# Two layers of a hybrid decoder trunk: every second pair of gate and up tiles begins with its 256-wide products, and down products stand inside a pair

## The chip, the cores and the metric

The kernel runs on one core of one Trainium2 chip. The metric is the device time of one execution in microseconds (us); lower is better. Three runs of the kernel before took 1044.72, 1044.97 and 1044.98 us, so its median is 1044.97 us. The profile shows one more execution, which has its own time, 1044.58 us.

The core has five engines that each work through their own list of instructions in order and wait for each other through semaphores: TensorE (PE in the profile: matrix products into the banks of PSUM; PEld is its loading of the stationary operand), VectorE (DVE), ScalarE (ACT), GpSimd (POOL) and SyncE (SP, which here only issues transfers). Main memory is read and written by DMA.

## What is computed

```
def swiglu(x, w_gate, w_up, w_down):
    return (jax.nn.silu(x @ w_gate) * (x @ w_up)) @ w_down
...
    for l in range(DEPTH):
        h = h + 0.5 * swiglu(rms_norm(h, ffn1_norm[l]), ffn1_w_gate[l], ffn1_w_up[l], ffn1_w_down[l])
        h = h + hybrid_mixer(rms_norm(h, mix_norm[l]), ...)
        h = h + 0.5 * swiglu(rms_norm(h, ffn2_norm[l]), ffn2_w_gate[l], ffn2_w_up[l], ffn2_w_down[l])
```

There are 256 tokens of width 1024, two layers (DEPTH is 2), and a hidden width of 2816 in each of the four feed-forward blocks (FFNs). All inputs are float32. The mixer (three groups of attention heads) is not touched by the change.

## The kernel before

Every float32 matrix is used as the sum of two parts in a reduced float32 format: the high part is the rounded value, the low part what is left. A product of two such matrices is three products: high by high, high by low, low by high.

**An FFN.** The hidden width is cut into 22 tiles of 128 (`NF`), counted by `f`. For each `f` there is a gate product (1024 by 128 weights against the tokens) and an up product of the same size; both have their own PSUM bank of 512 columns. Eight products that take the high weights as stationary operand and stream 512 columns (the tokens' high parts and their low parts side by side) fill the whole bank; these are the "wide" ones. Eight more, with the low weights and 256 columns (the tokens' high parts), add into the first half; these are the "narrow" ones. ScalarE then copies the second half of the bank out (`summed`, L434), VectorE adds the first half to it (L435), and from there the bank is free. Gate: times `norm.rb` (L439), a tanh on ScalarE (L441), two VectorE steps (`silu`, L458 and L459). Up: copy and add as before, times the gate (L446), then the high part (`hh`, L449) and the low part (`hl`, L452) of hidden tile `f`.

**The down product.** `down(k)` takes hidden tile `k` and its 128 rows of down weights and adds into four banks of tag "acc": 12 products of 512 columns, in the order high weights by `hh`, low weights by `hh`, high weights by `hl` for each bank. It runs four tiles late (`DOWN_LAG` is 4): beside pair `f` stands `down(f - 4)`. The last four are done in `tail` (or, in the very last FFN, in `finish`), bank after bank.

**Order.** The order of every engine's work is the order in which the program emits it. `Pair` (two weight tiles, two banks) emits gate wide, up wide, gate narrow, up narrow (`both`). Pairs are used from `f` = 2 on; in the first FFN from `f` = 6 on (`PAIR_FROM`), where tiles before stand singly (`proj`). In the loop over `f`, `both` comes first, then the gate's copy and the tanh, a `W.pump()`, then `down(f - DOWN_LAG)`, another pump, then the rest of the gate and the up side.

**Weights.** `Weights` loads raw float32 tiles through SP's queue (five buffers). A `pump` emits one high part on ScalarE (L117, tag "wh") and the low part of the unit before it on VectorE (L121, tag "wl"); eight buffers each. Units are taken in the order gate, up, down. So ScalarE and VectorE do two things in one list: they empty PSUM for the tile at hand, and they split weights for tiles to come. In the last two tiles (`late` in `hidden`) the pumps come after `hl`.

**Banks.** There are four banks of tag "gu", taken in turn, so pair `f` writes the banks that pair `f - 2` has left. In the first FFN, after `f` = 8, `aside` (`before_mixer`) takes two of them for two transposes (L177), and pair 9 then gets the banks of pair 8.

Of the kernel before, what the change touches and what calls it, by code (L numbers as in the profile page):

```python
# [21 lines left out]
KT = D // P  # L22
# [13 lines left out]
DOWN_LAG = 4  # L36
# [105 lines left out]
def kernel(ctx: ExitStack, tc: tile.TileContext, x, ffn1_norm, ffn1_w_gate, ffn1_w_up, ffn1_w_down,  # L142
# [17 lines left out]
    def bank(tag):  # L160
        return psum.tile([P, 512], F32, name="ps_" + tag, tag=tag)
# [43 lines left out]
    W = Weights(tc, raw_pool, split_pool)  # L205
# [87 lines left out]
    def mm(o, l, r, start, stop):  # L293
        T.matmul(o, l, r, start=start, stop=stop, skip_group_check=True)  # L294
# [64 lines left out]
    def tokens(o, q, hid, w, start, stop, cols=slice(0, 512)):  # L359

        t, c = q % 2, q // 2
        mm3(o, [h[:, t * P:(t + 1) * P] for h in hid], [v[:, 0, 512 * c + cols.start:512 * c + cols.stop] for v in w],
            start, stop)
# [8 lines left out]
    def ffn(norm, nxt, aside=None, g0=None):  # L372
        hid = {}

        def down(k):
            w = W.take()
            for q in range(4):
                tokens(acc[q], q, hid[k], w, k == 0, False)
            del hid[k]
# [16 lines left out]
        def proj(between=None, after=0, tag="gu"):  # L396


            w = W.take()
            ps = bank(tag).rearrange("p (a b) -> p a b", a=2)  # L400
            for k in range(KT):
                mm(ps, w[0][:, k], norm.x[:, k], k == 0, False)
            for k in range(KT):
                mm(ps[:, 0], w[1][:, k], norm.h[:, k], False, k == KT - 1)
                if between and k == after:
                    between()
            return ps

        class Pair:
# [11 lines left out]
            def narrow(self, ks):  # L421
                for w, ps in zip(self.ws, self.ps):
                    for k in ks:
                        mm(ps[:, 0], w[1][:, k], norm.h[:, k], False, k == KT - 1)

            def both(self, ks=range(KT)):
                self.wide(ks)
                self.narrow(ks)
                return self.ps

        def summed(ps):

            o = tmp(S)
            A.copy(o, ps[:, 1])  # L434
            V.tensor_tensor(o, ps[:, 0], o, op=ALU.add)  # L435
            return o

        def gated(t_):
            V.tensor_tensor(t_, t_, norm.rb, op=ALU.mult)  # L439
            th = tmp(S)  # L440
            A.activation(th, t_, AF.Tanh, scale=0.5)  # L441
            return t_, th

        def hidden(f, t_, th, u, pumps=1):
            late = f >= NF - 2
            V.tensor_tensor(t_, u, t_, op=ALU.mult)  # L446
            hh = hp.tile([P, S], F32R, name="hh", tag="hh")
            hl = hp.tile([P, S], F32R, name="hl", tag="hl")
            (V.tensor_copy if late else A.copy)(hh, t_)  # L449
            if not late:  # L450
                W.pump(pumps)
            V.tensor_tensor(hl, t_, hh.bitcast(F32), op=ALU.subtract)  # L452
            if late:
                W.pump(pumps)
            hid[f] = (hh, hl)

        def silu(t_, th):
            V.scalar_tensor_tensor(t_, th, 1.0, t_, op0=ALU.add, op1=ALU.mult)  # L458
            V.tensor_tensor(t_, t_, norm.rb, op=ALU.mult)  # L459

        first = g0 is not None
        early = {}
        if first:
# [4 lines left out]
            u1 = proj(norm.broadcast, 6)  # L468
# [25 lines left out]
        for f in range(1, NF):  # L494
            last = f == NF - 1
            paired = f >= (PAIR_FROM if first else 2)
            if paired:
                g, u = Pair().both()
            else:
                g, u = early[f] if f in early else proj(), u1 if f == 1 else None  # L500
            t_, th = gated(summed(g))
            if not last:
                W.pump()
            if f >= DOWN_LAG:
                down(f - DOWN_LAG)
                if not last:
                    W.pump()
            silu(t_, th)
            hidden(f, t_, th, summed(u or proj()), 3 if last else 1)
            if f == 8 and aside:  # L510
                aside()
# [567 lines left out]
    def before_mixer(l):  # L1079
        if l == 0:  # L1080
            turn_gains(1)
            turn_gains(2)
            V.tensor_copy(identr, ident)
            V.memset(causal[:, P:2 * P], 0.0)
            for t in range(2):
                V.tensor_scalar(causal[:, 2 * t * P:(2 * t + 1) * P], future, NEG, None, op0=ALU.mult)
        mixer_tables(l)
# [4 lines left out]
    norm = Norm(0, 0)  # L1092
# [52 lines left out]
    for l in range(DEPTH):  # L1145
        norm = ffn(norm, lambda: Norm(1, l), lambda: before_mixer(l), g0 if l == 0 else None)
        norm = mixer(l, norm, lambda: Norm(2, l))
        norm = ffn(norm, (lambda: Norm(0, l + 1)) if l + 1 < DEPTH else None)
# [35 lines left out]
```

## Time and profile before

| what | us |
|---|---|
| median of three runs | 1044.97 |
| the profiled execution, its time | 1044.58 |
| its span, first to last instruction | 1042.8 |
| PE busy | 1036.8 |
| DVE busy | 810.9 |
| ACT busy | 588.8 |
| the longest idle time of PE that the waits view shows inside the four FFNs | 0.6 |

The page of the profile gives busy times and shares of the span; groups of instructions stand as line, engine, operation, out<-in and count. In a timeline a row is a run of equal instructions: its start and its length in us, the engine, the line, what is written and read, the count, and in brackets the idle time of the engine before it with what ended it. The ends of matrix products are modelled, and products overlap, so that the distance between the starts of two rows, not the length of one, is the time that PE spent on the first.

### The profile page before, as it was taken

The page shows a single profiled execution, that of the slowest core. Times are in us where ns is not written, and L with a number is a line of the kernel's source. Part 1 is how long each engine was busy: PE and PEld are TensorE (multiplying, and loading weights), DVE is VectorE, ACT ScalarE, POOL GpSimd, SP SyncE. Part 2 cuts the span into 40 slices and gives each one's busy share as a digit, 9 for nine tenths or more (in the row PEclk, how much of TensorE's full clock was granted, in tenths as well). Part 3 has the DMA queues.
Part 4 walks back from the last instruction along what each step waited for, and adds up shares of the span by engine and source line. Part 5 has one row for each costly group of instructions (what it writes and reads, how often), then busy time and mean ns, then how long its engine had stood idle before and what let it go on. Part 6 is the DMA issues. An engine that isn't in the chain of part 4 may idle for free.

```text
span 1042.8 us, 15029 instructions
## 1 busy us (share of the span) xinstructions
PE 1036.8 (99%) x5667; PEld 900.4 (86%) x5667; DVE 810.9 (78%) x1536; ACT 588.8 (56%) x1047; POOL 143.5 (14%) x173
## 2 busy tenths in 40 slices
PE   9999999999999999999999999999999999999998
PEld 8888888898888888888888888888988888888887
DVE  4997777789876897777779777777898768877775
ACT  6665555667754665455466545547667555655551
POOL 1003000167700000000000210002765000000000
PEclk9999999999999999999999999999999999999999
DMA  9675555455441364554646574555455214574631
GB/s 326 213 242 177 194 207 170 157 196 192 149 137 41 122 236 169 201 192 171 202 162 203 170 240 159 205 164 192 162 186 178 81 60 153 193 240 151 214 121 40
DMA packets 130905, 181.68 MB, mean 174 GB/s; under 512 B 7009, under 2 KB 104721, under 8 KB 130833
## 3 DMA queue, kind: packets, MB, share of 16 engines
q1 hardware_dynamic: 130512, 180.65, 51.1%
q8 instruction: 44, 0.72, 0.3%
q14 instruction: 29, 0.23, 0.1%
q10 hardware_dynamic: 320, 0.08, 0.0%
HBM read 179.67 MB, written 1.05 MB: 173 GB/s over the span
## 4 chain that ended last, share of the span: by engine, by line
PE 92%; DVE 4%; ACT 2%; DMA 1%; issue 1%; SPq 0%; ACTq 0%
PE ps_gu L294 61%; PE ps_acc L294 28%; ACT wh L117 2%; DVE wl L121 1%; PE ps_acc L329 1%; DVE tmp L435 1%; PE ps_gu L943 1%; DMA trunk<-in_x_dram 1%; PE ps_gu L1045 1%; DVE tmp L459 0%; DVE tmp L446 0%; DVE tmp L439 0%; DVE tmp L458 0%; PE ps_acc L644 0%; ACT tmp L434 0%
## 5 line engine op out<-in xcount | busy, mean ns | idle before, releaser
L121 DVE TENSOR_TENSOR wl<-raw,wh 128x1024 fp32r<-128x1024 f32 (+2 forms) x343 | 416.5, 1220 | 26.4 <-ACT wh L117 26.1
L117 ACT CAST wh<-raw 128x1024 fp32r<-128x1024 f32 (+2 forms) x343 | 346.1, 1036 | 5.2 <-PE ps_gu L294 4.8
L294 PE MATMUL ps_gu<-xhl,wh 128*128 128x512 f32 (+1 forms) x1408 | 336.2, 389 | 1.2 <-DVE tmp L435 1.2
L294 PEld LDWEIGHTS ps_gu<-xhl,wh 128*128 128x128 f32 x1408 | 261.4, 188 | 55.5 <-DVE tmp L435 2.9
L294 PEld LDWEIGHTS ps_gu<-xhl,wl 128*128 128x128 f32 x1400 | 180.7, 191 | 7.2
L294 PE MATMUL ps_gu<-xhl,wl 128*128 128x256 f32 x1400 | 184.6, 283 | 0.0
L294 PE MATMUL ps_gu<-wh,xhl 128*128 128x512 f32 (+2 forms) x512 | 158.5, 379 | 0.0
L435 DVE TENSOR_TENSOR tmp<-ps_gu,tmp 128x256 f32<-128x256 f32 x175 | 73.6, 421 | 105.1 <-ACT tmp L434 104.9
L294 PE MATMUL ps_acc<-wh,hh 128*128 128x512 f32 (+1 forms) x352 | 137.7, 391 | 0.0
L294 PE MATMUL ps_acc<-wl,hh 128*128 128x512 f32 (+1 forms) x352 | 137.4, 390 | 0.0
L294 PE MATMUL ps_acc<-wh,hl 128*128 128x512 f32 (+1 forms) x352 | 136.5, 388 | 0.0
L434 ACT COPY tmp<-ps_gu 128x256 f32<-128x256 f32 x175 | 63.8, 365 | 92.4 <-PE ps_gu L294 91.9
L294 PEld LDWEIGHTS ps_gu<-wh,xhl 128*128 128x128 f32 x512 | 94.8, 188 | 14.5
L449 ACT CAST hh<-tmp 128x256 fp32r<-128x256 f32 x80 | 32.5, 407 | 125.9 <-DVE tmp L446 125.9
L294 PE MATMUL ps_gu<-wl,xhl 128*128 128x512 f32 (+2 forms) x256 | 95.7, 374 | 0.0
L441 ACT ACTIVATE tmp<-tmp 128x256 f32<-128x256 f32 x88 | 36.8, 418 | 82.0 <-DVE tmp L439 82.0
L305 POOL TENSOR_TENSOR y_n<-msq,minus_half 128x2 f32<-128x2 f32 x6 | 7.7, 1280 | 540.4 <-DVE msq L304 540.4
L294 PEld LDWEIGHTS ps_acc<-wh,hl 128*128 128x128 f32 x352 | 66.1, 188 | 14.1
L294 PEld LDWEIGHTS ps_acc<-wh,hh 128*128 128x128 f32 x352 | 66.4, 189 | 11.7
L294 PEld LDWEIGHTS ps_acc<-wl,hh 128*128 128x128 f32 x352 | 66.4, 189 | 10.8
L294 PEld LDWEIGHTS ps_gu<-wl,xhl 128*128 128x128 f32 x256 | 48.2, 188 | 6.6
L318 ACT ACTIVATE xhl<-ps_acc,gT 128x256 fp32r<-128x256 f32 x48 | 19.0, 474 | 37.5 <-PE ps_acc L329 37.0
(221 smaller groups left out, 1019.4 us busy)
## 6 DMA issues: line engine op xcount, KB each, us to landing
raw<-in_ffn_w_down_dram SPq DMA_DIRECT2D x44, 1024.0 KB, 5.0
raw<-in_ffn_w_gate_dram SPq DMA_DIRECT2D x43, 1024.0 KB, 6.9
raw<-in_ffn_w_up_dram SPq DMA_DIRECT2D x43, 1024.0 KB, 7.1
raw<-in_w_in_dram SPq DMA_DIRECT2D x24, 1024.0 KB, 5.0
raw<-in_w_out_dram SPq DMA_DIRECT2D x8, 1024.0 KB, 4.8
raw<-in_w_in_dram SPq DMA_DIRECT2D x4, 768.0 KB, 5.1
raw<-in_w_in_dram SPq DMA_DIRECT2D x4, 656.0 KB, 5.2
trunk<-in_x_dram SPq DMA_DIRECT2D x4, 256.0 KB, 5.1
```

Source lines behind the costliest of these rows:

```text
L117: self.nc.scalar.copy(hv, src)
L121: (engine or self.nc.vector).tensor_tensor(lv, self.srcs[self.n_low], hv.bitcast(F32), op=ALU.subtract)
L294: T.matmul(o, l, r, start=start, stop=stop, skip_group_check=True)
L305: G.tensor_tensor(y, dst, minus_half[:, :n], op=ALU.pow)
L318: A.activation(self.h[:, m], src, AF.Copy, scale=gT[:, self.col + m:self.col + m + 1])
L329: T.transpose(ps[:, i, t * P:(t + 1) * P], trunk[:, t, (2 * mp + i) * P:(2 * mp + i + 1) * P], ident)
L434: A.copy(o, ps[:, 1])
L435: V.tensor_tensor(o, ps[:, 0], o, op=ALU.add)
L441: A.activation(th, t_, AF.Tanh, scale=0.5)
L449: (V.tensor_copy if late else A.copy)(hh, t_)
L943: T.transpose(b[:, j * P:(j + 1) * P], pj[i][:, j * P:(j + 1) * P], ident)
L1045: T.transpose(b[:66, i * S + t * P:i * S + (t + 1) * P], src[t][:, 2 * hp_ + i, :], ident)
```

## The change

`Pair` gets a second way to run, `swapped`: gate narrow, up narrow, then something in between, then gate wide, up wide. Pairs with an odd `f` use it, with the down products in between; pairs with an even `f` run wide, then the down products, then narrow. Pair 21, the last, has its down products behind it as before. Where there is no `down` yet (`f` below 4) nothing stands in between. The lists of the other engines keep their order: ScalarE, VectorE, GpSimd and SP get the same instructions in the same order as before.

```diff
@@ class Pair @@
+            def swapped(self, between):
+
+                for w, ps in zip(self.ws, self.ps):
+                    for k in range(KT):
+                        mm(ps[:, 0], w[1][:, k], norm.h[:, k], k == 0, False)
+                between()
+                for w, ps in zip(self.ws, self.ps):
+                    for k in range(KT):
+                        mm(ps, w[0][:, k], norm.x[:, k], False, k == KT - 1)
+                return self.ps
@@ the loop over f @@
             paired = f >= (PAIR_FROM if first else 2)
-            if paired:
-                g, u = Pair().both()
+
+            def lagging():
+                if f >= DOWN_LAG:
+                    down(f - DOWN_LAG)
+
+            if not paired:
+                g, u = early[f] if f in early else proj(), u1 if f == 1 else None
+            elif f % 2:
+                g, u = Pair().swapped(lambda: None if last else lagging())
             else:
-                g, u = early[f] if f in early else proj(), u1 if f == 1 else None
+                p = Pair()
+                p.wide(range(KT))
+                lagging()
+                p.narrow(range(KT))
+                g, u = p.ps
             t_, th = gated(summed(g))
             if not last:
                 W.pump()
-            if f >= DOWN_LAG:
-                down(f - DOWN_LAG)
-                if not last:
-                    W.pump()
+            if not paired or last:
+                lagging()
+            if f >= DOWN_LAG and not last:
+                W.pump()
             silu(t_, th)
```

## Prediction

> **What bounds the kernel now.** I read the page first (busy times, granted clock, chain that ended last), then the waits of PE, then the chain in order of time.
>
> ```profile
> span 1042.8 us, 15029 instructions
> PE 1036.8 (99%) x5667; PEld 900.4 (86%) x5667; DVE 810.9 (78%) x1536; ACT 588.8 (56%) x1047; POOL 143.5 (14%) x173
> PEclk9999999999999999999999999999999999999999
> PE 92%; DVE 4%; ACT 2%; DMA 1%; issue 1%; SPq 0%; ACTq 0%
> PE ps_gu L294 <- DVE tmp L435: 1.2, 3, 0.6
> ```
>
> PE is busy all the time at the full granted clock. In the four FFNs it waits only three times, 1.2 us in all, each time for VectorE to empty a "gu" bank (L435). So time can be won only by making PE's products closer, and any wait put into PE's list is paid in full.
>
> ```profile
> 557.67 5.54 PE ps_gu L294 x32
> 563.21 2.75 PE ps_acc L294 x12
> 565.95 5.54 PE ps_gu L294 x32
> ...
> 565.79 3.79 PE L294 MATMUL ps_gu<-xhl,wh 128*128 128x512 f32 x16
> 569.42 2.08 PE L294 MATMUL ps_gu<-xhl,wl 128*128 128x256 f32 x16
> 571.33 0.40 PE L294 MATMUL ps_acc<-wh,hh 128*128 128x512 f32 x1
> 572.49 0.39 PE L294 MATMUL ps_acc<-wh,hl 128*128 128x512 f32 x1
> 574.08 3.79 PE L294 MATMUL ps_gu<-xhl,wh 128*128 128x512 f32 x16
> ```
>
> The chain: a period of 8.28 us, 32 products of a pair and 12 of a down, without a gap. Timeline of PE: 16 wide products take 569.42 - 565.79 = 3.63 us (0.227 each), 16 narrow ones 571.33 - 569.42 = 1.91 us (0.119 each), 12 down products 574.08 - 571.33 = 2.75 us. The last seven of these take 1.59 us, 0.227 each; the first five, behind the narrow ones, 1.16 us, 0.025 us more than five at 0.227. That is the price of a step from narrow to wide.
>
> Next, how far the other engines are from holding PE up.
>
> ```profile
> 570.63 0.37 ACT L434 COPY tmp<-ps_gu 128x256 f32<-128x256 f32 x1
> 571.84 1.22 DVE L121 TENSOR_TENSOR wl<-raw,wh 128x1024 fp32r<-128x1024 f32 x1
> 577.21 0.42 DVE L452 TENSOR_TENSOR hl<-tmp,hh 128x256 fp32r<-128x256 f32 x1
> 578.86 0.37 ACT L434 COPY tmp<-ps_gu 128x256 f32<-128x256 f32 x1 [1.30 <-PE ps_gu L294]
> ```
>
> The gate's eight narrow products end at 569.42 + 0.95 = 570.37; ScalarE copies 0.26 us later, and all that the two engines do for this tile ends 7.0 us behind that copy (577.63). Then ScalarE waits for PE's next gate tile. So in the steady state they follow PE, with 1.2 us to spare in 8.28. They also split weights: counted in the order of units, the low part at 571.84 is the gate tile of the pair that starts at 582.4, ready more than 9 us ahead.
>
> **The change part by part.** No product is added or removed; ACT, DVE, POOL and SP keep their lists, so no transfer passes another.
>
> Width steps: two pairs had two steps from narrow to wide, now one. The first FFN has 8 such doubles with downs (pairs 6 to 21), the other three 9 each (4 to 21): 35 x 0.025 = -0.9 us. Bounds: 0 (if the step costs the same wherever it stands, and something else makes it) and -0.9; I take -0.9, the measured row.
> [...]
>
> What moves is the moment at which banks are full and wanted. Even pair, from its start: gate complete after wide, down and eight narrow products, 3.63 + 2.72 + 0.95 = 7.30 us, where it was 3.63 + 0.95 = 4.58: 2.7 us later. Odd pair: narrow, down, eight wide = 1.91 + 2.75 + 1.81 = 6.47 us, 1.9 us later. So gates come 7.4 and 9.1 us apart in turn instead of 8.28; the 7.0 us of work behind a copy still fits. Weights are then ready up to 2.7 us later and wanted up to 3.6 us earlier: of more than 9 us some 3 are left, so this costs nothing in the steady state; if that cover were gone, each pair would pay the lack. But in an odd pair the up tile's bank is now wanted 8 narrow products (0.95 us) behind the gate's, where it was 8 wide ones (1.81 us): 0.86 us earlier. Three places have no slack for all this.
>
> *Pair 3 of the later three FFNs.* No down stands here yet.
>
> ```profile
> 357.37 0.42 DVE L435 TENSOR_TENSOR tmp<-ps_gu,tmp 128x256 f32<-128x256 f32 x1 [0.23 <-ACT tmp L434]
> 358.16 4.02 PE L294 MATMUL ps_gu<-xhl,wh 128*128 128x512 f32 x16
> 359.60 0.42 DVE L435 TENSOR_TENSOR tmp<-ps_gu,tmp 128x256 f32<-128x256 f32 x1
> 542.92 2.00 PE L294 MATMUL ps_gu<-xhl,wh 128*128 128x512 f32 x8
> 545.34 2.11 PE L294 MATMUL ps_gu<-xhl,wh 128*128 128x512 f32 x8 [0.41 <-DVE tmp L435]
> 873.42 4.02 PE L294 MATMUL ps_gu<-xhl,wh 128*128 128x512 f32 x16
> ```
>
> Pair 3 starts at 358.16; its up tile gets the bank that VectorE leaves at 359.60 + 0.42 = 360.02, almost exactly when the up's wide products came (358.16 + 1.81 = 359.97). In the third FFN it came 0.41 us idle too late already; 873.42 is the twin of 358.16 (both 16 in 4.02). VectorE works off the two pairs before here and does not follow PE, so the bank does not come free earlier. The up's narrow products stop PE, and the gate's wide ones are queued behind them: 0.86 us in each of three FFNs, +2.6. Bounds: 0.8 and 1.0 each (the first product after a wait comes a little slower: 545.34 to its successors).
>
> *Pair 9 of the first FFN*, which gets the banks of pair 8 at once.
>
> ```profile
> 65.73 3.79 PE L294 MATMUL ps_gu<-xhl,wh 128*128 128x512 f32 x16
> 69.35 2.08 PE L294 MATMUL ps_gu<-xhl,wl 128*128 128x256 f32 x16
> 74.33 2.11 PE L294 MATMUL ps_gu<-xhl,wh 128*128 128x512 f32 x8
> 77.04 2.11 PE L294 MATMUL ps_gu<-xhl,wh 128*128 128x512 f32 x8 [0.61 <-DVE tmp L435]
> 71.88 0.36 ACT L434 COPY tmp<-ps_gu 128x256 f32<-128x256 f32 x1
> 76.57 0.42 DVE L435 TENSOR_TENSOR tmp<-ps_gu,tmp 128x256 f32<-128x256 f32 x1
> ```
>
> Gate 8 was copied at 71.88, its up's bank free at 76.99, and PE waited until 77.04. Now pair 8 (start 65.73, wide until 69.35) has the down before its narrow products: 69.35 + 2.72 + 0.95 + 0.26 = 73.28, so the copy slides by 1.4 us and the bank's release to 78.4. Up 9's narrow products want it at 74.33 + 0.95 = 75.3 and wait there until 78.4. Then narrow 0.96, down 2.75, wide 3.63: pair 9 ends at 85.7, with the slow restart 85.8. Before: 77.04 + 1.95 + 1.91 + 2.75 = 83.65. So +2.1 (bounds 1.8 and 2.4).
>
> *The end of all four FFNs.* Pair 20 is even, pair 21 has no down inside.
>
> ```profile
> 171.29 0.37 ACT L434 COPY tmp<-ps_gu 128x256 f32<-128x256 f32 x1 [1.36 <-PE ps_gu L294]
> 177.52 1.22 DVE L121 TENSOR_TENSOR wl<-raw,wh 128x1024 fp32r<-128x1024 f32 x1
> 179.58 0.37 ACT L434 COPY tmp<-ps_gu 128x256 f32<-128x256 f32 x1 [3.44 <-PE ps_gu L294]
> 179.98 0.42 DVE L435 TENSOR_TENSOR tmp<-ps_gu,tmp 128x256 f32<-128x256 f32 x1 [1.24 <-ACT tmp L434]
> 183.74 3.49 DVE L121 TENSOR_TENSOR wl<-raw,wh 128x1024 fp32r<-128x1024 f32 x3
> 185.35 0.39 PE L294 MATMUL ps_acc<-wl,hh 128*128 128x512 f32 x1
> ```
>
> Gate 20 was copied at 171.29; VectorE's work for it ended 7.45 us later (177.52 + 1.22 = 178.74), then it stood idle 1.24 us for gate 21. Now the copy comes 2.72 us later, and that work ends at 181.46. Gate 21 is complete earlier than before (narrow 1.91 + eight wide 1.81 instead of 3.63 + 0.95), so VectorE, not PE, is last: L435 starts at 181.4 instead of 179.98. All behind it slides by 1.4 to 1.5 us, the first of the three low parts at 183.74 too. That one is down tile 21's, ready at 184.96 and used at 185.35: 0.39 us spare. PE waits 1.4 - 0.39 = 1.0 to 1.1 us, with a slower restart 1.15. Queued behind it are all the rest of the tail and, through the residual, the next stage's norm. Four FFNs: +4.6 (bounds 4.0 and 5.2; the last FFN ends in the same order of units).
>
> Sum: -0.9 + 2.6 + 2.1 + 4.6 = +8.4 us on the profiled time 1044.58 (its span is 1042.8; 1.8 lies around it): 1053.0. The median is 0.39 above that execution, so 1053.4.
>
> **The rivals.**
>
> *The tail does not wait* (the two engines gain on the shorter list of pairs 20 and 21, and the low part comes in time): -0.9 + 2.6 + 2.1 = +3.8, 1048.8. For it: ScalarE has 3.44 us idle there. Against: VectorE's list is the one without room, 1.24 + 0.39 = 1.63 us against 2.72.
>
> *The closer products win.* PE's waits are where DVE is late by a fixed list; if releases and low parts came 1.5 us earlier than I read them, all three places would be covered and only the width steps would be left: -0.9, 1044.1. It decides where the slack exceeds the slide: 0.86 us at pair 3, 1.5 at the tail. Against: the trace has PE waiting there before the change, 0.41 and 0.61 us.
>
> *The clock drops.* PE would stand still some 2.9 us in pair 9 and be granted a lower clock afterwards.
>
> ```profile
> 0.98 3.36 PE L294 MATMUL ps_gu<-ones 128*128 128x128 f32 x14 [0.98 <-POOL minus_half L183]
> ```
>
> After idling, PE's first 14 products took (3.36 us, modelled end included) over 0.2 us each for 128 columns, where 256 columns take 0.119 later: half speed or less over at least 3.4 us, so 1.7 to 3.4 us more, say 2.5: 1055.9. Against: idle times of 0.61 us left the clock at full; none so long is in the trace.
> [...]
>
> **How the numbers follow.** Forecast 0.70, own range 1051.8 to 1054.8 (sum of the bounds, softened); tail in time or half in time 0.12; clock drop 0.06; weights short in some steady pair, up to 3 us more, 0.05; closer products win 0.07. From 1048.3 to 1056.4 holds all but the last of these and the ends of the others, about 0.86. What this measurement can tell from no change is about 0.2%, 2.1 us: slower 0.93; of the last case, which lies at -0.9 us, same 0.05, and faster 0.02 if a width step costs over twice what I read.
>
> **What would show it.** Right: in the waits of PE for L435 four waits instead of three, one near 3 us at 75 to 78 us, three of 0.8 to 1.3 us at the third pair of the later FFNs; four new waits of about 1 us for DVE wl L121 at the tails; a double period of 16.55 instead of 16.57 us. Wrong: no wait for L121; a clock under 1.00 behind the wait at 78; idle time in the middle of an FFN, which would mean that weights came late.

## The result and the profile after

The changed kernel took 1055.33 us (median of five executions: 1053.44, 1055.14, 1055.33, 1055.44, 1055.58) against 1044.72 us for the kernel before beside it: a ratio of 1.0100, 95% interval 1.0089 to 1.0111. It is slower by 10.6 us. The profiled execution took 1055.44 us.

The page of the changed kernel: span, busy times, clock by slices, and the chain that ended last, by engine.

```profile
span 1053.7 us, 14998 instructions
PE 1038.4 (99%) x5667; PEld 901.4 (86%) x5667; DVE 809.8 (77%) x1536; ACT 589.0 (56%) x1047; POOL 141.7 (13%) x173
PEclk9999999999999999999999999999999999999999
PE 91%; DVE 6%; ACT 2%; issue 1%; DMA 1%; SPq 0%; ACTq 0%; DVEq 0%
```

The products are the same 5667, and DVE's and ACT's busy times are the same within 1.2 us. PE is busy 1.6 us longer, and the span has grown by 10.9 us. So about nine microseconds are waits, and 1.6 are products that went slower. The chain shows where: DVE went from 4% to 6% of it. The strip of the clock shows nothing; a slice of it is 26 us wide.

The waits of PE after the change (what was waited for: us in total, times, longest):

```profile
PE ps_gu L294 <- DVE tmp L446: 6.3, 5, 2.9
PE ps_acc L294 <- DVE wl L121: 3.6, 4, 0.9
```

L446 is the addition that empties a "gu" bank (L435 before). It held PE up for 1.2 us in three waits and now does so for 6.3 us in five. The four waits for a weight's low part (L121) are new, one for each FFN. Eight of the nine stand at the three places that the prediction names. The ninth, 0.2 us for a single tile of the first FFN at 24.23, was there before as well (at 24.02), so that five waits stand where the prediction counted on four. Comparing the start of the same product in both traces gives the price of each place.

| place | before to after, us |
|---|---|
| start of the kernel, up to its first FFN product | +0.2 |
| pair 9 of the first FFN | +3.87 |
| pair 3 of the later three FFNs | +0.85, +0.85, +1.12 |
| the four tails | +1.19 each |
| all other pairs together | -0.85 |
| sum | +10.8 |

*Pair 9 of the first FFN*, in the chain of waits of the changed kernel (start, length, what):

```profile
72.42 0.97 PE ps_gu L294 x8
...
73.47 0.38 ACT tmp L445
...
73.88 0.43 DVE tmp L446
...
75.27 0.94 ACT wh L117
...
76.24 1.23 DVE wl L121
...
78.26 0.34 DVE tmp L446
...
78.65 1.53 PE ps_gu L294 x8
80.18 4.02 PE ps_acc L294 x12
84.20 7.26 PE ps_gu L294 x32
```

Read it downwards. Gate 8's narrow products end at 73.39; its copy, addition and tanh follow; then the high part (0.94) and the low part (1.23) of a weight for a later tile, which the pumps emit, stand in the same two lists, then silu, and only the addition for up 8 at 78.26 frees the bank that up 9 needs. PE stands still from 75.7 to 78.65. The row behind it is the surprise: twelve down products take 4.02 us where twelve took 2.75 before. The timeline of PE and its windows (length; busy time of PE, PEld, DVE, ACT and POOL, each with a count; then PE's clock, the DMA share and GB/s) show why:

```profile
78.65 1.53 PE L294 MATMUL ps_gu<-xhl,wl 128*128 128x256 f32 x8 [2.95 <-DVE tmp L446]
79.98 0.63 PE L294 MATMUL ps_acc<-wh,hh 128*128 128x512 f32 x1
80.40 0.63 PE L294 MATMUL ps_acc<-wl,hh 128*128 128x512 f32 x1
```

```profile
75.93:79.34 3.41, 0.69 (x5) 0.69 (x6) 3.03 (x6) 1.75 (x4) 0.05 (x1) 1.00 0.84 286
79.34:82.76 3.42, 3.42 (x12) 2.84 (x11) 2.27 (x8) 1.10 (x2) 3.34 (x8) 0.50 0.12 29
82.76:86.17 3.41, 3.41 (x16) 2.78 (x16) 0.00 (x0) 0.05 (x1) 2.62 (x9) 1.00 0.02 5
```

From 79.34 to 82.76 the granted clock is one half, and products of 512 columns stand 0.42 us apart instead of 0.23. The wait itself had been forecast; the lower clock behind it had not.

*The tail of the first FFN* (timeline of the changed kernel):

```profile
189.05 3.49 DVE L121 TENSOR_TENSOR wl<-raw,wh 128x1024 fp32r<-128x1024 f32 x3
190.32 0.50 PE L294 MATMUL ps_acc<-wl,hh 128*128 128x512 f32 x1 [0.90 <-DVE wl L121]
190.66 0.40 PE L294 MATMUL ps_acc<-wh,hl 128*128 128x512 f32 x1
```

The first of the three low parts is ready at 189.05 + 1.22 = 190.27, and PE takes it up at 190.32, after 0.90 us of idle time. Before, it was ready 0.39 us ahead of its use.

*Pair 3 of the second FFN*:

```profile
361.32 3.03 PE L294 MATMUL ps_gu<-xhl,wl 128*128 128x256 f32 x24
365.13 1.22 PE L294 MATMUL ps_gu<-xhl,wl 128*128 128x256 f32 x8 [0.79 <-DVE tmp L446]
```

Twenty-four narrow products are pair 2's sixteen and gate 3's eight; the up's eight stand 0.79 us behind them for their bank.

*The steady middle of the third FFN* (chain of waits):

```profile
603.14 7.25 PE ps_gu L294 x32
610.39 2.72 PE ps_acc L294 x12
613.11 3.83 PE ps_gu L294 x32
616.94 2.75 PE ps_acc L294 x12
619.69 7.25 PE ps_gu L294 x32
```

Wide products of two pairs now stand together (7.25 us), and narrow ones (3.83 us). Two pairs take 619.69 - 603.14 = 16.55 us without a gap; before, two periods of 8.28 to 8.29. The 12 down products behind wide ones take 2.72, those behind narrow ones 2.75: the closer products that the change brings are there, and are worth 0.02 to 0.03 us in two pairs.

### The profile page after: what moved, and what is told of

Same layout as the page of the kernel before. It is cut to its first block, busy times and chain, and to the rows that moved or that the text cites. A ratio compares the mean times of both kernels' runs of the same rounds, so it can differ in the third digit from the quotient of the medians.

```text
span 1053.7 us, 14998 instructions
## 1 busy us (share of the span) xinstructions
PE 1038.4 (99%) x5667; PEld 901.4 (86%) x5667; DVE 809.8 (77%) x1536; ACT 589.0 (56%) x1047; POOL 141.7 (13%) x173
## 4 chain that ended last, share of the span: by engine, by line
PE 91%; DVE 6%; ACT 2%; issue 1%; DMA 1%; SPq 0%; ACTq 0%; DVEq 0%
PE ps_gu L294 60%; PE ps_acc L294 28%; DVE wl L121 2%; ACT wh L117 1%; PE ps_acc L329 1%; DVE tmp L446 1%; PE ps_gu L965 1%; DVE tmp L470 1%; DMA trunk<-in_x_dram 1%; DVE tmp L469 1%; PE ps_gu L1067 0%; DVE tmp L450 0%; DVE tmp L457 0%; ACT tmp L452 0%; ACT tmp L445 0%
## 5 line engine op out<-in xcount | busy, mean ns | idle before, releaser
L121 DVE TENSOR_TENSOR wl<-raw,wh 128x1024 fp32r<-128x1024 f32 (+2 forms) x343 | 416.2, 1219 | 26.4 <-ACT wh L117 26.2
L294 PE MATMUL ps_gu<-xhl,wh 128*128 128x512 f32 (+1 forms) x1408 | 329.6, 389 | 0.2 <-DVE tmp L446 0.2
L294 PE MATMUL ps_gu<-xhl,wl 128*128 128x256 f32 x1400 | 180.2, 284 | 6.1 <-DVE tmp L446 6.1
L294 PEld LDWEIGHTS ps_gu<-xhl,wl 128*128 128x128 f32 x1400 | 176.2, 192 | 11.1 <-DVE tmp L446 6.9
L446 DVE TENSOR_TENSOR tmp<-ps_gu,tmp 128x256 f32<-128x256 f32 x175 | 73.5, 420 | 117.3 <-ACT tmp L445 117.0
L457 DVE TENSOR_TENSOR tmp<-tmp 128x256 f32<-128x256 f32 x88 | 37.5, 426 | 3.0
```

The costliest lines, as they stand in the source:

```text
L121: (engine or self.nc.vector).tensor_tensor(lv, self.srcs[self.n_low], hv.bitcast(F32), op=ALU.subtract)
```

## Experiments

Edits are against the changed kernel unless stated, and all times are medians. "Old order" means wide, wide, narrow, narrow and then the downs, as before the change.

**Each place by itself.** The first four kernels give the old order back to the pairs of one place. `PLACE` stands for `f == 3` in e1, `first and f in (8, 9)` in e2, `f == 20` in e3, and all of these in e4.

```diff
+            elif PLACE:
+                g, u = Pair().both()
             elif f % 2:
@@
-            if not paired or last:
+            if not paired or last or PLACE:
                 lagging()
```

e1, pair 3 (its rival counts 68 pairs of new order; there are 73, which moves the rival by less than 0.1 us):

> The changed kernel (median 1055.3 us), with pair 3 of the later three FFNs put back to the old order (wide, narrow). Theory of three places: the waits at pair 3 go (in the trace of the changed kernel they cost 0.85, 0.85 and 1.12 us against before), all else stays: 2.8 us less, 1052.5 us. Rival, the new order is slower in every pair alike (10.6 us over 68 pairs of new order, 0.16 us each): three pairs give back 0.5 us, 1054.8.

e2, pairs 8 and 9 of the first FFN:

> The changed kernel, with pairs 8 and 9 of the first FFN put back to the old order. Theory of three places: the wait of 2.95 us for the bank of up 8 falls back to 0.6, and as PE no longer stands still so long, the granted clock stays at 1.00 behind it: 3.9 us less, 1051.4 us, and all rounds alike. If the stretch at half clock has another cause than this wait: 2.1 us less, 1053.2, and the clock still drops. Rival, every pair alike: two pairs give back 0.3 us, 1055.0.

e3, pair 20:

> The changed kernel, with pair 20 of all four FFNs put back to the old order (wide, narrow, down behind). Theory of three places: gate 20 is complete 2.7 us earlier again, VectorE's list at the tail is no longer late, and the four waits for the last low part (1.19 us each) go: 4.8 us less, 1050.5 us. Rival, every pair alike: four pairs give back 0.6 us, 1054.7.

e4, all three places:

> All three put back at once: pairs 3 and 20 in every FFN where they stand in the loop, and pairs 8 and 9 of the first. The other pairs keep the new order. Theory of three places: only the fewer steps between widths are left, about 0.02 us in each double pair: 0.5 to 0.8 us below before, 1044.1 us with before at 1044.7. Rival, every pair alike: 60 pairs of the new order still cost 9 us, 1054.

| kernel | us | against 1055.33 | ratio to the kernel before |
|---|---|---|---|
| e1, pair 3 | 1052.88 | -2.45 | 1.0078 (1.0064 to 1.0092) |
| e2, pairs 8 and 9 | 1051.07 | -4.26 | 1.0061 (1.0047 to 1.0074) |
| e3, pair 20 | 1050.47 | -4.86 | 1.0056 (1.0043 to 1.0068) |
| e4, all three | 1044.01 | -11.32 | 0.9995 (0.9986 to 1.0003) |

The three places give -11.57 one by one and -11.32 together, so they add up, and only the width steps are left. e1 gives back less than the 2.8 us expected: 0.28 us of the price in the last FFN stays with the old pair 3, because a tanh is late there as well. The waits of PE say the same, each kernel losing the waits of its own place. In e2 the longest for L446 is down from 2.9 to 1.3:

```profile
PE ps_gu L294 <- DVE tmp L446: 3.7, 5, 1.3
```

In e3 the row for L121 is gone, and that for L446 stays at 6.3 us; product by product, its tails cost nothing against the kernel before.
In e4 the waits for L446 are back at 1.2 us in three. What is left of the change there, the width steps, is 0.6 us under the kernel before (1044.61 beside it), and its interval reaches over 1.

**Which pair carries the price.** In e5 the even pairs begin with their narrow products and the odd ones with their wide ones. Pairs 3 and 9 then begin with their wide products, and pair 21 has its wide ones first as well.

```diff
-            elif f % 2:
-                g, u = Pair().swapped(lambda: None if last else lagging())
+            elif f % 2 == 0:
+                g, u = Pair().swapped(lagging)
             else:
                 p = Pair()
                 p.wide(range(KT))
-                lagging()
+                if not last:
+                    lagging()
```

> The other parity: pairs with an even f begin with their narrow products and have the down products before the wide ones, pairs with an odd f run wide, down, narrow. As many pairs of each kind, as many down products inside pairs, as many steps between widths as in the changed kernel. Theory of three places: pair 3 begins wide as before (no loss), the copy of gate 8 is 0.5 us late instead of 1.4 and pair 9 wants its second bank 1.81 us in (wait 0.5 us longer than before, no clock drop), gate 20 is 1.85 us late of which 1.63 are covered (0.1 to 0.3 us at each tail), steps -0.8: 1045.0 us with before at 1044.6. Rival, the new order costs in every pair alike: 1055.

1045.91 us, ratio 1.0014 (1.0005 to 1.0023): 9.4 us less than the changed kernel, with the same kind and number of alternating pairs. So alternating costs nothing by itself here; it is the parity that asks early for a late bank. It is 0.9 us more than was expected. The longer wait at pair 9 came out as forecast, and its place costs 0.55 us against the kernel before; each tail costs 0.36 where 0.1 to 0.3 was expected, and this is part of the 0.9.

```profile
PE ps_gu L294 <- DVE tmp L446: 1.8, 3, 1.2
```

```profile
77.28 2.09 PE L294 MATMUL ps_gu<-xhl,wh 128*128 128x512 f32 x8 [1.17 <-DVE tmp L446]
...
185.23 0.39 PE L294 MATMUL ps_acc<-wh,hh 128*128 128x512 f32 x1
185.68 0.50 PE L294 MATMUL ps_acc<-wl,hh 128*128 128x512 f32 x1
186.02 0.39 PE L294 MATMUL ps_acc<-wh,hl 128*128 128x512 f32 x1
```

Pair 9 waits 1.17 us instead of 0.61. At 185.23 a distance of 0.45 us stands where the product before it has 0.23, and the next is 0.34: a wait of 0.22 us and 0.11 of a slower restart. This wait has no row in the waits view, because idle time counts from the modelled end of the product before: 185.23 + 0.39 = 185.62, only 0.06 us ahead of the next start. Such waits are seen only in the distances.

**The two halves of pair 9's place.** e6 gives the old order back to pair 8 alone, e7 to pair 9 alone (`PLACE` is `first and f == 8`, then `first and f == 9`).

> The changed kernel, with pair 8 of the first FFN in the old order and pair 9 in the new one. The second bank of pair 9 is free at 77.0 us and wanted at 75.3, so that PE is idle about 1.5 us instead of 2.95. Theory that the clock drops only when most of one of the periods of 3.41 us in which it is set (the length of the one slow stretch in the trace) is idle: no drop, 0.9 us over before in this place, 1052.3 us in all. Rival, any idle time of 1.5 us or more drops it: 1.7 us more, 1054.0, and a stretch at half clock in the trace.

> The changed kernel, with pair 8 of the first FFN in the new order and pair 9 in the old one. The second bank is free at 78.4 us and wanted at 76.15, so that PE is idle about 2.1 us. The wait costs 1.4 us more than before: 1052.8 us without a drop of the clock. A period of 3.41 us can hold at most 62% of idle time here (85% in the changed kernel); if that is enough to drop the clock, some rounds lie 1.7 us higher, near 1054.5.

e6 took 1052.53 us (ratio 1.0077, 1.0065 to 1.0090) and e7 1054.09 (1.0088, 1.0075 to 1.0102). With the old pair 8 the wait is 1.5 us and the mean clock of all its executions at least 0.999. With the old pair 9 the wait is 2.1 us; three of its four executions show 0.998 and 1053.81 to 1054.38 us, and the fourth 1.000 and 1052.62. One of e6's five executions took 1054.11 us at a mean clock of 1.000; no profile of it exists, and the reason stays open. The windows of e7:

```profile
75.31:78.72 3.41, 1.38 (x6) 0.78 (x5) 3.00 (x5) 2.21 (x4) 0.00 (x0) 1.00 0.99 335
78.72:82.13 3.41, 3.38 (x8) 2.70 (x9) 2.86 (x9) 1.35 (x2) 1.41 (x4) 0.50 0.19 50
```

Only 2.0 of 3.41 us are idle in the first window, and the second is at half the clock all the same.

**The clock by itself.** e10 and e11 are the changed kernel again, unaltered, to see how executions differ.

> The changed kernel itself, unaltered, to see another execution's clock. In its rounds the mean clock was 0.998 in two executions (1055.14 and 1055.44 us) and 1.000 in three (1053.44, 1055.33, 1055.58). Theory: the clock changes only on a grid of 3.413 us; an execution loses about 1.7 us either to a half-clock window behind pair 9's wait (mean clock 0.998), or, where that wait lies across a border of the grid, nothing there, but then the clock may rise one window later at the start. So: either a half clock window that begins at the first border behind a window that was mostly idle, or no such window and no window that holds more than about 2 us of the wait. Rival: the 1.7 us have another cause than the clock, and an execution without a half-clock window is as long between pair 8 and pair 10 as one with it.

> The same as the run before it, one more execution. Theory: from the start of pair 9 (74.5) to that of pair 10 it takes 13.2 us with a half-clock window behind the wait and 11.5 us without one. Rival: 13.2 in both.

e10 took 1055.76 us and e11 1053.86. Their windows on the grid of the clock's changes, in steps of 3.413 us (in the trace of the changed kernel the clock changes at 4.25 and at 79.34 us, 22 such steps apart), e10 first:

```profile
77.00:80.41 3.41, 1.54 (x11) 1.45 (x12) 3.34 (x7) 1.74 (x4) 0.69 (x1) 1.00 0.57 181
80.41:83.83 3.42, 3.42 (x10) 2.64 (x9) 1.43 (x8) 0.26 (x1) 3.26 (x11) 0.50 0.09 22
```

```profile
76.82:80.23 3.41, 1.62 (x11) 1.53 (x12) 3.34 (x7) 1.74 (x4) 0.70 (x1) 1.00 0.54 174
80.23:83.64 3.41, 3.41 (x17) 2.81 (x16) 1.36 (x7) 0.18 (x1) 3.25 (x11) 1.00 0.11 26
```

Both executions wait 2.95 us, and in both the wait lies across a border of the grid: in e10 it ends at 78.87, so it began at 75.92, with a border at 77.00; in e11 it goes from 75.66 to 78.61, with a border at 76.82. In e10 the window with the larger part of it has PE busy for 1.54 us, and half the clock follows; in e11 it is busy for 1.62 us, and the clock stays. The chains, e10 and then e11, give the price:

```profile
78.87 1.22 PE ps_gu L294 x8
80.09 4.34 PE ps_acc L294 x12
84.44 7.26 PE ps_gu L294 x32
```

```profile
78.61 1.21 PE ps_gu L294 x8
79.83 2.75 PE ps_acc L294 x12
82.57 7.25 PE ps_gu L294 x32
```

From the restart to the first wide product it is 84.44 - 78.87 = 5.57 us with the drop and 82.57 - 78.61 = 3.96 without: 1.61 us. Compared product by product with the kernel before, pair 9's place costs e11 2.27 us, and every other place what it costs in the table above, within 0.1 us. So the rival, another cause than the clock, falls.

**Filling the wait.** In e12 the down products of pair 9 in the first FFN alone stand between gate narrow and up narrow.

```diff
-            def swapped(self, between):
+            def swapped(self, between, split=False):
                 for w, ps in zip(self.ws, self.ps):
                     for k in range(KT):
                         mm(ps[:, 0], w[1][:, k], norm.h[:, k], k == 0, False)
-                between()
+                    if split and ps is self.ps[0]:
+                        between()
+                if not split:
+                    between()
@@
-                g, u = Pair().swapped(lambda: None if last else lagging())
+                g, u = Pair().swapped(lambda: None if last else lagging(), first and f == 9)
```

> Pair 9 of the first FFN alone gets another order: gate narrow, down, up narrow, gate wide, up wide; all else as in the changed kernel. The 12 down products fill 2.75 us of the wait for the up's bank. Theory: the wait shrinks from 2.95 to 0.2 to 0.5 us, no window of the grid is mostly idle, so the clock stays at full: 1055.3 - 2.5 - 1.7 = 1051.1 us, mean clock 1.000 in all rounds. Rival: the loss of 1.7 us beside the wait isn't the clock's answer to the wait: 1055.3 - 2.5 = 1052.8. If the down's low weights are not split yet at 75.4 us, a wait for DVE wl L121 shows there and less is saved.

1051.45 us (1050.74 to 1053.03), ratio 1.0066 (1.0050 to 1.0083), mean clock 1.000 in every execution. Two rows of its timeline:

```profile
78.66 0.39 PE L294 MATMUL ps_acc<-wh,hl 128*128 128x512 f32 x1
79.25 1.22 PE L294 MATMUL ps_gu<-xhl,wl 128*128 128x256 f32 x8 [0.21 <-DVE tmp L449]
```

The bank is as late as before (L449 is the same addition there), but PE works on until 79.04 and waits 0.21 us. The place now costs 0.44 us less than in the kernel before instead of 3.87 more.

**What a width step costs.** In e9 (against the kernel before) pairs 11 to 19 run gate wide, gate narrow, up wide, up narrow, which adds one step from narrow to wide to each: 36 more.

```diff
+            def apart(self):
+                for w, ps in zip(self.ws, self.ps):
+                    for k in range(KT):
+                        mm(ps, w[0][:, k], norm.x[:, k], k == 0, False)
+                    for k in range(KT):
+                        mm(ps[:, 0], w[1][:, k], norm.h[:, k], False, k == KT - 1)
+                return self.ps
@@
-                g, u = Pair().both()
+                g, u = Pair().apart() if 11 <= f < 20 else Pair().both()
```

> The kernel before, with pairs 11 to 19 of all four FFNs run as gate wide, gate narrow, up wide, up narrow: one more step from narrow to wide and one back in each, nothing else. If a step to wide costs 0.025 us and the step back saves 0.007 (the first narrow product stands 0.113 us apart instead of 0.120): the period of a pair grows from 8.29 to 8.31 us, 36 pairs, +0.6 us. Rival, the width of the neighbour costs nothing: 8.29 and no difference.

1045.49 us, ratio 1.0007 (0.9997 to 1.0016): the times alone don't settle it. In the trace the last products are 0.62 us later against the first ones than before: 0.017 us for a step to wide and the step back together, where 0.025 - 0.007 = 0.018 was expected. A pair's period is 616.38 - 608.07 = 8.31 us:

```profile
608.07 5.56 PE ps_gu L294 x32
613.63 2.75 PE ps_acc L294 x12
616.38 5.56 PE ps_gu L294 x32
```

**A version that keeps what is good.** e8 alternates only in the middle of an FFN, with e5's parity, and keeps the old order at all three places. Pair 3 there runs gate before up (`apart`, as in e9), which asks for the up's bank later, and `aside` takes its two banks two tiles later.

```diff
+            two = (12 if first else 6) <= f < 18
@@
-            elif f % 2:
-                g, u = Pair().swapped(lambda: None if last else lagging())
+            elif not two and f == 3:
+                g, u = Pair().apart()
+            elif not two:
+                g, u = Pair().both()
+            elif f % 2 == 0:
+                g, u = Pair().swapped(lagging)
@@
-            if not paired or last:
+            if not two:
                 lagging()
@@
-            if f == 8 and aside:
+            if f == 10 and aside:
                 aside()
```

> A version meant to beat both: new order in the other parity, and only from pair 12 to 17 in the first FFN and 6 to 17 in the others; pair 3 of the others runs gate wide, gate narrow, up wide, up narrow, so that its second bank is wanted 0.95 us later; the transposes of the mixer's gains stand behind pair 10 instead of 8, where VectorE has caught up. Theory of three places: no wait at a tail, none at pair 3 (before: 0.1, 0.6, 0.1 us and slow restarts of 0.1), none or a short one behind the transposes (before 0.9), 17 fewer steps between widths (-0.35): 2.2 us below before, 1042.4 us at 1044.6. Rival, every pair alike: 20 double pairs of the new order cost 5 us, 1050.

1042.22 us, ratio 0.9978 (0.9969 to 0.9988): 2.4 us under the kernel before (1044.66 beside it) and 13.1 under the changed one. The chain by engine on its page, and the only row for L454, the addition that empties a bank there, among its waits of PE (it is the wait of the single tile near 24 us):

```profile
PE 98%; DMA 1%; DVE 0%; ACT 0%; SPq 0%; issue 0%
```

```profile
PE ps_gu L294 <- DVE tmp L454: 0.2, 1, 0.2
```

DVE's 4% of the chain have become 0%. Most of the gain isn't the change's: the waits of the kernel before, 0.6 us at pair 9 and at pair 3 of the third FFN 0.4, are gone as well. In its trace pairs 8 to 11 with the transposes give 0.9 us, the three pairs 3 together 1.0, and the width steps 0.35, each close to what was expected; its start is 0.3 us earlier than that of the kernel before, and two executions of the changed kernel differ by as much (pair 9 begins at 74.71 us in e10 and at 74.44 in e11).

## The prediction, step by step

*What bounds the kernel*: right. Every microsecond of wait in PE's list was paid in full, and e1 to e4 add up.

*Width steps, -0.9*: the way was right, and the size in part by luck. All other pairs together gave -0.85. But a steady double pair gains 0.02 us, not 0.025: with a step to wide goes a step back to narrow, which gave 0.007 us (its first product stands 0.113 us from the next one instead of 0.120) and which the prediction left out. 35 times 0.02 is 0.7; the rest was won elsewhere, part of it at pair 4 of the later FFNs (0.05 us each).

*Pair 3, +2.6*: right, with +2.82 measured. Twice it was 0.85; in the third of the three 1.12, because the tanh of pair 1 began 0.28 us later there. That lies outside the bound of 1.0. It is no accident of one execution: the seven traces in which pair 9 of the first FFN begins with its narrow products (the changed kernel, e1, e3, e6, e10, e11, e12) all show this late tanh in the last FFN, and the seven others don't. What links the two stays open.

*Pair 9, +2.1*: right as far as it goes. Where the clock stays at full (e11) the place costs 2.27, inside the bounds. In the profiled execution it costs 3.87, for the lower clock behind the wait, which the step left out.

*The tails, +4.6*: right, 4 x 1.19 = 4.76. The list of VectorE was late by what was read, and nothing but the spare 0.39 us was taken off it. The rival in which the tail doesn't wait fell with the four rows for L121.

*The clock drops*: this was put down as a rival at 0.06, in place of the forecast; it happened on top of it. It is the one step that failed: from "idle times of 0.61 us left the clock at full" the prediction took a wait of 2.9 us to be too short as well, and no row of the kernel before showed that. The lost 1.6 us lie just under the 1.7 to 3.4 that the rival gave as its price.

*The sum*: +8.4 forecast, 1053.4. The measured 1055.33 lies above the forecast's own range, 1051.8 to 1054.8; the wider range up to 1056.4 holds it because of the rival of the clock. Without the drop, e11's own time is 1053.86 us, 9.3 over the profiled execution of before; of the 0.9 us between them, some 0.2 each come from pair 3, pair 9, the tails and the start of the kernel. With the drop it is 1055.4. Of seven executions of the changed kernel three show a mean clock of 0.998 (1055.14, 1055.44, 1055.76) and two show 1.000 and a time that is 1.3 to 2.3 us less (1053.44, 1053.86). Two more, 1055.33 and 1055.58, show 1.000 and the longer time; they weren't profiled, and where they lost it stays open. A late start could be it, as in e3's profiled execution: there the second 14 products of 128 columns take 3.15 us (5.96 to 9.11), where they take 1.97 in the kernel before (5.33 to 7.30), and the first row of four high-weight products starts 1.95 us later (10.80 against 8.85). Its mean clock is 1.000 all the same; the window 0.84:4.25 of the changed kernel shows 1.00 too, with products of 128 columns 0.21 us apart instead of 0.11.

*Closer products win, weights short*: neither. The alternating middle has the predicted period of 16.55 us without an idle stretch.

## What to carry to other kernels

When an order of products is changed, price it at the places where the pattern begins and ends and where a bank changes hands: here the steady middle had slack, and the edges decided. Count from both sides of a bank: the later its last product, the later the engines that empty it, and the earlier the next tile's first product, the longer PE stands (at pair 3 of the second FFN the bank is wanted 0.86 us earlier, and PE waits 0.79 us). Price a new wait on TensorE with and without a lower clock behind it: in these runs 2.1 us (e7) and 2.95 us (the changed kernel, e10) had 3.4 us at half the clock behind them, 1.61 us more by e10 against e11; the same 2.95 us in e11 and 1.5 us in e6 had none. Other products put into the wait saved both here (e12).

## What the runs showed of the hardware

In the profiled execution of the changed kernel the granted clock rose at 4.25 us, fell to one half at 79.34 and was full again from 82.76: 75.09 us, 22 times 3.413, and then 3.42. The stretches at half the clock in e1 (78.68 to 82.09), e7 (78.72 to 82.13) and e10 (80.41 to 83.83) are as long, 3.41 to 3.42 us. Their place against the kernel differs between executions: in e10, the same kernel, the clock fell 1.07 us later than in the changed kernel's own trace, and pair 9 went on after its wait only 0.22 us later (78.87 against 78.65).

In the 3.41 us before a fall PE was busy for 0.49 us (e1), 0.69 (the changed kernel), 1.38 (e7) and 1.54 (e10). Behind windows of the same length with 1.62 (e11), 1.69 (the end of the changed kernel, 1048.73 to 1052.14) and 1.80 us (e3) the clock stayed at 1.00. An estimate from these seven windows is that the border lay between 1.54 and 1.62 us here; the runs do not show more of its cause. The same wait of 2.95 us cost 1.61 us more in e10 than in e11.

At the start of the changed kernel products of 128 columns stand 0.21 us apart up to 3.91 us, and 0.11 us apart from 5.21 on. In e3 a row of four takes 0.71 us at 9.11 and 0.36 us at 11.36.

In two tails the product behind the first one after a wait came late as well, 0.34 us behind it (190.66 - 190.32 in the changed kernel at a clock of 1.00, 186.02 - 185.68 in e5), where later ones stand 0.23 us apart (191.13 - 190.90, 186.25 - 186.02).
